# Two-layer hybrid decoder trunk on one core: the steps of the attention tasks one half unit further apart, branch B pairs every four half units

## The chip, the cores and the metric

The kernel runs on one core of a Trainium2 chip. The metric is device time in microseconds (us) of one execution, lower is better. PE is the matrix engine, DVE the vector engine, ACT the scalar engine, POOL and SP the two others; each works through its own list of instructions in the order in which the program wrote them, and waits for the others by semaphores.

## What is computed

Two layers, 256 tokens, model width 1024. Each layer is a half-step SwiGLU, a mixer, and a second half-step SwiGLU, each with a residual and a layer norm:

```python
for l in range(DEPTH):
    x = layer_norm(ALPHA * x + 0.5 * swiglu(x, ffn1_up[l], ffn1_down[l]), ln1_g[l], ln1_b[l])
    mix = hybrid_mixer(x, positions, w_in[l], ...)
    x = layer_norm(ALPHA * x + mix, ln2_g[l], ln2_b[l])
    x = layer_norm(ALPHA * x + 0.5 * swiglu(x, ffn2_up[l], ffn2_down[l]), ln3_g[l], ln3_b[l])
```

```python
s = jnp.einsum('bnqgrd,bnkgd->bngrqk', qb, kk) * (hd ** -0.5)     # banded_attention
s = jnp.where(mask[None, :, None, None], s, -jnp.inf)
m = jnp.max(s, axis=-1)                    # branch B: maximum with the sink as well
e = jnp.exp(s - m[..., None])
den = jnp.sum(e, axis=-1)                  # branch B: plus exp(sink - m)
o = jnp.einsum('bngrqk,bnkgd->bnqgrd', e, vv) / den_t[..., None]
lse = jnp.transpose(m, (0, 1, 4, 2, 3)) + jnp.log(den_t)
```

The mixer has three branches that are gated, summed and projected: A (12 heads, three dilated windows whose outputs are combined by their softmax denominators), B (16 query heads on 2 key heads, window 128, with a sink in the denominator) and C (retention, 8 heads). All is float32.

## The kernel before

Nearly all time goes to products of the activations with weights. Each weight is loaded as float32 (`ws`) and split into a high part `wh` (ACT, line 279) and a low part `wl` (DVE, line 289, `ws` minus `wh`); three products of 256 or 512 columns (line 320) then make one product of full precision. The weights are cut into units of up to four 128-row tiles by 512 columns, and each unit is worked through in two halves (`mm_unit(u, 0)` and `mm_unit(u, 1)`, for the two halves of the output). One such half is a half unit: 24 matmuls of 256 columns or 12 of 512. Within a unit `run` writes, in this order: the first half's matmuls and a `tick`; `hi_until`, which issues the `wh` of the unit three further on to ACT; the second half's matmuls and a `tick`; `lo_until`, which issues the `wl` of that same unit to DVE. So `wh` stands behind the steps of a first half's tick on ACT, and `wl` waits for that `wh`.

The attention is hung between the half units by hand. Each task is a generator, and one `tick` steps it to its next `yield`; a `yield` more puts what follows one half unit later in all five lists. The ends of a product chunk (`done_...`) are written right after the tick: the rotation of queries and keys (`rope`, four to five DVE instructions, lines 523 to 543) for the chunks `cq`, `ck`, `bq`, `bkv`, `aqk`; copies and a Silu on ACT for others.

- `b_pair` (branch B, eight pairs of heads in a layer, called here (0,0) to (1,3)): scores on PE into `S` (line 634), then on DVE the mask with a running maximum (639) and the negated maximum `bnm` (786), on ACT the exponentials (643) and the sink's (791). A `yield`. On DVE the reciprocal of the denominators `bden` (793, 794), on ACT the scaling of the probabilities (798). A `yield`. Four transposes on PE into `T` and their copy by ACT (625, 626). A `yield`. The last two. For every second pair a further `yield` and the product with the values, `U` (814), for two pairs, with its copy (816).
- `a_quad` (branch A, three in a layer): near scores of two head pairs (two yields behind each), far scores with their mask and exponentials, a `yield`, the merge of the two sums (`top`, `af`, `aw`, `fn`, lines 712 to 724), a `yield`, the scaling (730 and 734), a `yield`, three steps of transposes (625, 626, into `T` and `S`), two yields, the values (`U`, 748).

`T` and `U` have one buffer each in PSUM, `S` two. `an`, where the probabilities lie, has two buffers, `af` one. A pair starts when three half units have passed since the last start, a quad when no pair and no quad is under way.

Half units are counted here from the one after which the scores of pair (0,0) stand: that is 0. Even ones are first halves of a unit (a `wh` follows), odd ones second halves (a `wl` follows).

```
kind    b_pair scores at           a_quad starts at   values of the last quad at
before  0 3 6 9 12 15 18 21        25 44 60           71
```

Of the kernel before, what the change touches and what calls it, by code (L numbers as in the profile page):

```python
# [161 lines left out]
class Kernel:  # L162
# [40 lines left out]
    def tick(self, half):  # L203
        self.pairs = self.step(self.pairs)
        alive = self.step(self.tasks[half])
        kind = self.waiting and self.waiting[0][0] <= self.now and self.waiting[0][2]
        if kind and {"two": half == 1, "pair": self.now >= self.last + 3, "quad": not self.pairs}[kind]:
            g = self.waiting.popleft()[1]
            next(g)
            (alive if kind == "two" else self.pairs).append(g)  # L210
            self.last = self.now
        self.tasks[half] = alive + self.fresh
        self.fresh = []
        self.now += 1
# [480 lines left out]
    def a_quad(self, s):  # L695
        nc = self.nc
        new = lambda n: self.sml.tile([128, 2, 2, 4], F32, name=n, bufs=2)
        near, far, moved, f, w = (new(n) for n in ("near", "far", "moved", "af", "aw"))

        places = [(slice(32 * r, 32 * r + 32), t, slice(64 * (r % 2) + 32 * t, 64 * (r % 2) + 32 * t + 32), r // 2)  # L700
                  for r in range(4) for t in range(2)]
        P = []
        for b in range(2):
            P.append(self.near_scores(s, b, near))
            yield
            yield
        for rows, t, to, rp in places:
            nc.gpsimd.tensor_copy(moved[to, :, rp], near[rows, :, t])
        F = self.far_scores(s, far)
        yield  # L710
        top = self.sml.tile([128, 2, 4], F32, name="top", bufs=2)
        nc.vector.tensor_tensor(top, moved[:, 0], far[:, 0], op=OP.min)
        for g, x in enumerate((moved, far)):
            nc.vector.tensor_tensor(f[:, g], top, x[:, 0], op=OP.subtract)
        nc.scalar.activation(f, f, AF.Exp)
        for g, x in enumerate((moved, far)):
            nc.vector.tensor_tensor(w[:, g], f[:, g], x[:, 1], op=OP.mult)
        nc.vector.tensor_tensor(top, w[:, 0], w[:, 1], op=OP.add)
        nc.vector.reciprocal(top, top)
        for g in range(2):  # L720
            nc.vector.tensor_tensor(f[:, g], f[:, g], top, op=OP.mult)
        fn = self.sml.tile([128, 2, 4], F32, name="fn", bufs=2)
        for rows, t, to, rp in places:
            nc.scalar.activation(fn[rows, t], f[to, 0, rp], AF.Copy)  # L724
        yield
        for b in range(2):
            for e in range(2):
                for t in range(2):
                    sl = P[b][:, e, self.TILES[t]]
                    nc.scalar.activation(sl, sl, AF.Copy, scale=fn[:, t, 2 * b + e:2 * b + e + 1])  # L730
        for h in range(4):
            for rp in range(2):
                sl = F[:, 256 * h + 128 * rp:256 * h + 128 * rp + 128]
                nc.scalar.activation(sl, sl, AF.Copy, scale=f[:, 1, rp, h:h + 1])  # L734
        yield
        for x, n in ((P[0], 6), (P[1], 6), (F, 8)):
            x = x.rearrange("p e k -> p (e k)") if n == 6 else x
            self.transpose_p(x, 0, 4)
            self.transpose_p(x, 4, n, spare=True)
            yield  # L740
        yield
        self.a_values(s, P, F)
# [31 lines left out]
    def b_pair(self, n, b):  # L774

        nc, l = self.nc, self.layer
        Sp = self.pair_scores(self.bq[n][:, b], self.kb[:, n])
        P = self.b_p[n, b] = self.probs((4 * n + b) % 3 == 2)
        mx, nm, den, es = (self.sml.tile([128, 2, 2], F32, name=x) for x in ("bmx", "bnm", "bden", "bes"))
        h = 8 * n + 2 * b  # L780
        for e in range(2):
            sk = self.sink[:, l, h + e:h + e + 1]
            for t in range(2):
                self.masked(P[:, e, self.TILES[t]], Sp[e][:, self.TILES[t]], self.mask[:, 512 - 128 * t:640], mx[:, e, t:t + 1])
            nc.vector.tensor_scalar(mx[:, e], mx[:, e], 0.125, sk, op0=OP.mult, op1=OP.max)
        nc.vector.tensor_scalar(nm, mx, -1.0, None, op0=OP.mult)
        for e in range(2):
            sk = self.sink[:, l, h + e:h + e + 1]
            for t in range(2):
                self.exp(P[:, e, self.TILES[t]], nm[:, e, t:t + 1], den[:, e, t:t + 1])  # L790
            nc.scalar.activation(es[:, e], mx[:, e], AF.Exp, bias=sk, scale=-1.0)
        yield
        nc.vector.tensor_tensor(den, den, es, op=OP.add)
        nc.vector.reciprocal(den, den)
        for e in range(2):
            for t in range(2):
                sl = P[:, e, self.TILES[t]]
                nc.scalar.activation(sl, sl, AF.Copy, scale=den[:, e, t:t + 1])
        yield
        x = P.rearrange("p e k -> p (e k)")  # L800
        self.transpose_p(x, 0, 4)
        yield
        self.transpose_p(x, 4, 6)
        if b % 2 == 0:
            return
        yield
        U = self.p1.tile([128, 2, 256], F32, name="U")
        v = self.vb[:, :, 64 * n:64 * n + 64]
        for i in range(2):
            p = self.b_p[n, b - 1 + i]  # L810
            for j in range(2):
                for e in range(2):
                    u = U[64 * e:64 * e + 64, i]
                    nc.tensor.matmul(u[:, 128 * j:], v[:, j], p[:, e, 256 * j:256 + 128 * j], start=j == 0, stop=j == 1,
                                     skip_group_check=True)
        nc.scalar.activation(self.y[1][:, 4 * n + b - 1:4 * n + b + 1], U, AF.Copy)
        self.b_done += 1
# [279 lines left out]
```

## Time and profile before

| | |
|---|---|
| three runs | 1761.38, 1761.82 (median), 1762.82 us |
| the profiled execution | 1762.2 us, span 1760.0 us |
| PE busy | 1694.4 us, 96% of the span |
| PE's weight loads | 1543.4 us, 88% |
| DVE busy | 1067.1 us, 61% |
| ACT busy | 842.3 us, 48% |
| POOL busy | 96.1 us, 5% |
| mean granted clock of PE | 0.983 |

A share of busy time says which engine is nearest to its limit over the whole span. Which wait counts at a place is read from the list of waits, from the timeline of the engine that waits, and then from the timelines of those that it waits for.

### The profile page before, as it was taken

How to read it: one execution, taken by the hardware profiler on the slowest of the kernel's cores; microseconds unless marked ns; L12 is line 12 of the kernel's file. 1: busy time of each engine (PE TensorE's matmuls, PEld its weight loads, DVE VectorE, ACT ScalarE, POOL GpSimd, SP SyncE). 2: the span in 40 equal slices, each digit the busy share in tenths (PEclk: the TensorE clock that was granted, in tenths of full speed). 3: DMA queues.
4: the chain of work that ended last, by engine and by line, in shares of the span. 5: the costliest groups of instructions: out<-in, count | busy, mean ns of one | idle time of the engine just before them, and what ended most of it. 6: DMA issues, size and time to landing. Idle time of an engine off the chain costs nothing.

```text
span 1760.0 us, 29034 instructions
## 1 busy us (share of the span) xinstructions
PE 1694.4 (96%) x12325; PEld 1543.4 (88%) x12325; DVE 1067.1 (61%) x1536; ACT 842.3 (48%) x1207; POOL 96.1 (5%) x176
## 2 busy tenths in 40 slices
PE   9999999899988999999999999999999989999997
PEld 7998898788878998999899988978888889979985
DVE  5555677677564557555655546877666635675544
ACT  5444334675467444444344434366664574444431
POOL 0000001010210000000000000010102100000000
PEclk9999999999999999999999999999999999999998
DMA  7555543433443445555455465343344434555451
GB/s 288 210 185 194 207 169 125 142 135 138 161 159 117 180 180 192 209 210 204 165 188 206 176 222 193 144 144 120 132 144 156 156 144 180 194 185 213 172 206 48
DMA packets 49137, 303.38 MB, mean 172 GB/s; under 512 B 7024, under 2 KB 7280, under 8 KB 15088
## 3 DMA queue, kind: packets, MB, share of 16 engines
q1 hardware_dynamic: 44640, 294.12, 45.7%
q0 software_dynamic: 4224, 7.35, 1.2%
q8 instruction: 96, 1.57, 0.3%
q14 instruction: 33, 0.27, 0.0%
q10 hardware_dynamic: 144, 0.07, 0.0%
HBM read 297.31 MB, written 1.05 MB: 170 GB/s over the span
## 4 chain that ended last, share of the span: by engine, by line
PE 80%; DVE 9%; ACT 8%; issue 2%; DMA 0%; POOL 0%; SPq 0%; POOLq 0%; DVEq 0%; ACTq 0%
PE acc L320 75%; DVE wl L289 3%; ACT wh L279 2%; ACT an L643 1%; ACT af L643 1%; DVE an L639 1%; PE T L625 1%; PE S L634 1%; DVE af L639 1%; PE U L748 1%; ACT an L730 1%; ACT fn L724 1%; ACT af L734 1%; DVE rt L523 0%; DVE x L479 0%
## 5 line engine op out<-in xcount | busy, mean ns | idle before, releaser
L320 PE MATMUL acc<-xT,wh 128*128 128x256 f32 x4800 | 854.7, 281 | 0.0
L289 DVE TENSOR_TENSOR wl<-ws,wh 128x2048 fp32r<-128x2048 f32 (+1 forms) x277 | 615.5, 2241 | 215.2 <-ACT wh L279 213.5
L320 PEld LDWEIGHTS acc<-xT,wh 128*128 128x128 f32 x4800 | 740.7, 190 | 0.2
L320 PE MATMUL acc<-xT,wl 128*128 128x256 f32 x2400 | 683.3, 285 | 0.0
L279 ACT ACTIVATE wh<-ws 128x2048 fp32r<-128x2048 f32 (+1 forms) x277 | 518.8, 1874 | 249.8 <-PE acc L320 208.8
L320 PEld LDWEIGHTS acc<-xT,wl 128*128 128x128 f32 x2400 | 457.5, 191 | 8.2 <-issue 6.7
L320 PE MATMUL acc<-wh,xT 128*128 128x512 f32 (+1 forms) x832 | 265.9, 394 | 0.2
L320 PE MATMUL acc<-wh,hT 128*128 128x512 f32 x704 | 222.9, 396 | 0.0
L320 PEld LDWEIGHTS acc<-wh,xT 128*128 128x128 f32 x832 | 156.2, 190 | 37.3 <-issue 2.3
L320 PE MATMUL acc<-wl,xT 128*128 128x512 f32 (+1 forms) x416 | 162.2, 390 | 0.2 <-DVE wl L448 0.2
L320 PEld LDWEIGHTS acc<-wh,hT 128*128 128x128 f32 x704 | 132.6, 188 | 31.3
L320 PE MATMUL acc<-wl,hT 128*128 128x512 f32 x352 | 139.4, 396 | 0.0
L320 PE MATMUL acc<-slab,wh 128*128 128x256 f32 x704 | 123.8, 279 | 0.0
L490 DVE TENSOR_TENSOR h<-sa,acc 128x512 f32<-128x512 f32 x36 | 24.8, 688 | 154.2 <-PE acc L320 154.2
L320 PEld LDWEIGHTS acc<-slab,wh 128*128 128x128 f32 x704 | 107.2, 188 | 0.1
L320 PE MATMUL acc<-slab,wl 128*128 128x256 f32 x352 | 99.0, 281 | 0.0
L487 ACT ACTIVATE sa<-acc 128x512 f32<-128x512 f32 x36 | 21.5, 597 | 158.4 <-PE acc L320 158.4
L320 PEld LDWEIGHTS acc<-wl,xT 128*128 128x128 f32 x416 | 79.1, 190 | 16.4 <-DVE wl L448 0.5
L320 PEld LDWEIGHTS acc<-wl,hT 128*128 128x128 f32 x352 | 66.3, 188 | 15.5
L625 PE MATMUL T<-ident,an 128*128 128x128 f32 x120 | 26.5, 325 | 47.1 <-ACT an L730 26.3
L574 POOL DMA_DIRECT2D va<-slab x96 | 51.4, 538 | 324.6 <-ACT slab L570 319.7
L320 PEld LDWEIGHTS acc<-slab,wl 128*128 128x128 f32 x352 | 66.2, 188 | 1.6 <-issue 1.3
(177 smaller groups left out, 1242.3 us busy)
## 6 DMA issues: line engine op xcount, KB each, us to landing
ws<-in_w_dram SPq DMA_DIRECT2D x265, 1024.0 KB, 4.9
ws<-in_w_dram SPq DMA_DIRECT2D x12, 512.0 KB, 4.2
ws<-in_w_dram SPq DMA_DIRECT2D x12, 256.0 KB, 5.9
va<-slab POOLq DMA_DIRECT2D x96, 32.0 KB, 4.1
gain<-in_ln_g_dram SPq DMA_DIRECT2D x4, 512.0 KB, 5.8
gain<-in_ln_b_dram SPq DMA_DIRECT2D x4, 512.0 KB, 7.1
slab<-in_decay_dram POOLq DMA_DIRECT2D x4, 512.0 KB, 4.7
x<-in_x_dram SPq DMA_DIRECT2D x4, 256.0 KB, 5.8
```

What stands on the lines that cost most here:

```text
L279: self.nc.scalar.activation(wh[:, :n], self.staged[v][:, :n], AF.Copy)
L289: self.nc.vector.tensor_tensor(wl[:, :n], ws[:, :n], wh[:, :n].bitcast(F32), op=OP.subtract)
L320: nc.tensor.matmul(ps[:, c0:c1], a, b, start=first, stop=last, skip_group_check=len(parts) > 1)
L487: nc.scalar.activation(self.sa, ps, AF.Silu)
L490: nc.vector.tensor_tensor(h, self.sa, ps, op=OP.mult)
L574: nc.gpsimd.dma_start(self.vf[s][p0:p0 + 32, r], self.stage[r::4, t, g])
L625: nc.tensor.transpose(ps[:, 128 * (i - lo):128 * (i - lo) + 128], P[:, 128 * i:128 * i + 128], self.ident)
L634: self.nc.tensor.matmul(Sp[e][:, 128 * t:128 + 256 * t], q[r, 128 * t:128 * t + 128], k[r, :128 * t + 128], start=True, stop=True)
L639: self.nc.vector.tensor_tensor_reduce(out=P, in0=Sp, in1=mask, op0=OP.add, op1=OP.max, scale=1.0, scalar=-3e38, accum_out=mx)
L643: self.nc.scalar.activation(P, P, AF.Exp, bias=nm, scale=0.125, accum_out=den)
L724: nc.scalar.activation(fn[rows, t], f[to, 0, rp], AF.Copy)
L730: nc.scalar.activation(sl, sl, AF.Copy, scale=fn[:, t, 2 * b + e:2 * b + e + 1])
```

## The change

Five `yield`s are added and one number is raised.

```diff
-        if kind and {"two": half == 1, "pair": self.now >= self.last + 3, "quad": not self.pairs}[kind]:
+        if kind and {"two": half == 1, "pair": self.now >= self.last + 4, "quad": not self.pairs}[kind]:
...
         F = self.far_scores(s, far)
         yield
+        yield
         top = self.sml.tile([128, 2, 4], F32, name="top", bufs=2)
...
             nc.scalar.activation(fn[rows, t], f[to, 0, rp], AF.Copy)
         yield
+        yield
         for b in range(2):
...
                 nc.scalar.activation(sl, sl, AF.Copy, scale=f[:, 1, rp, h:h + 1])
+        yield
         yield
         for x, n in ((P[0], 6), (P[1], 6), (F, 8)):
...
             nc.scalar.activation(es[:, e], mx[:, e], AF.Exp, bias=sk, scale=-1.0)
         yield
+        yield
         nc.vector.tensor_tensor(den, den, es, op=OP.add)
...
                 nc.scalar.activation(sl, sl, AF.Copy, scale=den[:, e, t:t + 1])
         yield
+        yield
         x = P.rearrange("p e k -> p (e k)")
```

In a pair the scaling stands two half units behind the scores and not one, the first transposes four and not two; the step to the last transposes and the one to the values keep one half unit. In a quad the merge stands two behind the far scores, the scaling four and not two, the first transposes six and not three. Pairs start at 0, 4, 8, ... 28, quads at 34, 48 and 62, and the last quad's values stand at 76.

The lists of the two programs show what this moves. On ACT, around the last transposes of pair (0,3) and the values that need them (626: copies of transposes; 643, 791 or 794: exponentials of the next pair; 279: `wh`; 816 or 821: copy of the values' product). Before:

```order
L626 ACTIVATE an_3103<-T_3189 128x512
L626 ACTIVATE an_3103<-T_3222 128x256
L643 ACTIVATE an_3232,bden_3235<-an_3232,bnm_3234 128x128
L643 ACTIVATE an_3232,bden_3235<-an_3232,bnm_3234 128x256
L791 ACTIVATE bes_3236<-bmx_3233,sink_110 128x2
L643 ACTIVATE an_3232,bden_3235<-an_3232,bnm_3234 128x128
L643 ACTIVATE an_3232,bden_3235<-an_3232,bnm_3234 128x256
L791 ACTIVATE bes_3236<-bmx_3233,sink_110 128x2
L279 ACTIVATE wh_3258<-ws_3026 128x2048
L816 ACTIVATE y_2277<-U_3285 128x512
```

The same place now:

```order
L626 ACTIVATE an_3188<-T_3341 128x512
L643 ACTIVATE an_3353,bden_3356<-an_3353,bnm_3355 128x128
L643 ACTIVATE an_3353,bden_3356<-an_3353,bnm_3355 128x256
L794 ACTIVATE bes_3357<-bmx_3354,sink_110 128x2
L643 ACTIVATE an_3353,bden_3356<-an_3353,bnm_3355 128x128
L643 ACTIVATE an_3353,bden_3356<-an_3353,bnm_3355 128x256
L794 ACTIVATE bes_3357<-bmx_3354,sink_110 128x2
L279 ACTIVATE wh_3379<-ws_3150 128x2048
L626 ACTIVATE an_3188<-T_3406 128x256
L821 ACTIVATE y_2277<-U_3433 128x512
```

The copy of the last two transposes stood ahead of the next pair's exponentials and of a `wh`; now it stands behind both.

On ACT, in the second quad, from its far exponentials (643) to its scaling (715, 724 or 716, 725: the merge; 447: a split of branch B's result). Before:

```order
L643 ACTIVATE af,far<-af,far 128x128 x8
L279 ACTIVATE wh<-ws 128x2048
L715 ACTIVATE af<-af 128x16
L724 ACTIVATE fn<-af 32x4 x8
L730 ACTIVATE an<-an,fn 128x128
```

Now:

```order
L643 ACTIVATE af,far<-af,far 128x128 x8
L279 ACTIVATE wh<-ws 128x2048
L716 ACTIVATE af<-af 128x16
L725 ACTIVATE fn<-af 32x4 x8
L447 ACTIVATE slab<-y 128x512
L279 ACTIVATE wh<-ws 128x2048
L447 ACTIVATE slab<-y 128x512
L732 ACTIVATE an<-an,fn 128x128
```

A `wh` and two splits now stand between merge and scaling. On DVE, from the negated maximum of pair (0,3) (786 or 789) to its reciprocal (794 or 798), before:

```order
L786 TENSOR_SCALAR bnm<-bmx 128x4
L523 STREAM_SHUFFLE rt<-acc 128x512
L524 TENSOR_TENSOR rt<-acc,cos 128x512
L525 TENSOR_TENSOR rt<-rt,sin 128x512
L534 TENSOR_TENSOR slab<-rt 128x512
L289 TENSOR_TENSOR wl<-ws,wh 128x2048
L793 TENSOR_TENSOR bden<-bden,bes 128x4
L794 RECIPROCAL bden<-bden 128x4
```

Now:

```order
L789 TENSOR_SCALAR bnm<-bmx 128x4
L523 STREAM_SHUFFLE rt<-acc 128x512
L524 TENSOR_TENSOR rt<-acc,cos 128x512
L525 TENSOR_TENSOR rt<-rt,sin 128x512
L543 TENSOR_TENSOR slab<-rt 128x256 x2
L523 STREAM_SHUFFLE rt<-acc 128x512
L524 TENSOR_TENSOR rt<-acc,cos 128x512
L525 TENSOR_TENSOR rt<-rt,sin 128x512
L543 TENSOR_TENSOR slab<-rt 128x256 x2
L289 TENSOR_TENSOR wl<-ws,wh 128x2048
L797 TENSOR_TENSOR bden<-bden,bes 128x4
L798 RECIPROCAL bden<-bden 128x4
```

Both rotations of a chunk and a `wl` now stand between a pair's maximum and its reciprocal.

## Rows read from the trace of the kernel before

**Rows 1.** Busy time by stretch: PE, PEld, DVE, ACT, POOL, granted clock, DMA share, GB/s.

```profile
260.00:600.00 340.00, 315.18 (x2545) 284.38 (x2544) 220.28 (x485) 200.34 (x418) 39.83 (x76) 0.96 0.40 143
...
1130.00:1470.00 340.00, 314.91 (x2529) 283.98 (x2529) 219.66 (x484) 198.76 (x418) 39.86 (x76) 0.96 0.40 142
```

**Rows 2.** PE's waits over the whole span: us in total, times, longest.

```profile
PE T L625 <- ACT an L730: 26.3, 6, 4.5
PE T L625 <- ACT an L798: 12.6, 6, 2.5
PE T L625 <- ACT an L626: 7.7, 6, 1.5
```

**Rows 3.** Two stretches with waits, columns as in the first group.

```profile
360.00:380.00 20.00, 17.87 (x117) 14.34 (x116) 15.81 (x39) 12.04 (x33) 0.00 (x0) 1.00 0.41 155
...
420.00:440.00 20.00, 15.82 (x84) 13.71 (x83) 13.39 (x21) 14.83 (x33) 0.00 (x0) 0.83 0.41 149
```

**Rows 4.** The chain that ended last, first layer: start, us, what.

```profile
396.20 1.45 PE U L814 x16
...
411.01 1.10 PE S L678 x64
...
501.66 2.81 PE acc L320 x24
...
572.43 2.38 PE U L748 x48
```

**Rows 5.** The chain within 499 to 506 us: four transposes without a wait.

```profile
504.48 0.44 PE T L625 x4
```

**Rows 6.** Timeline of PE: scores of pair (0,0), first layer.

```profile
294.27 0.93 PE L634 MATMUL S<-kb,slab 64*128 64x128 f32 x8
```

**Rows 7.** Timeline of DVE around pair (1,0), 347.8 to 358.5 us.

```profile
345.68 2.29 DVE L289 TENSOR_TENSOR wl<-ws,wh 128x2048 fp32r<-128x2048 f32 x1 [3.43 <-ACT wh L279]
...
349.72 0.74 DVE L523 STREAM_SHUFFLE rt<-acc 128x512 f32<-128x512 f32 x1
...
352.75 0.16 DVE L793 TENSOR_TENSOR bden<-bden,bes 128x4 f32<-128x4 f32 x1
...
353.05 0.75 DVE L523 STREAM_SHUFFLE rt<-acc 128x512 f32<-128x512 f32 x1
...
356.09 2.28 DVE L289 TENSOR_TENSOR wl<-ws,wh 128x2048 fp32r<-128x2048 f32 x1
```

**Rows 8.** Timeline of ACT, the same pair.

```profile
351.98 1.91 ACT L279 ACTIVATE wh<-ws 128x2048 fp32r<-128x2048 f32 x1
...
354.27 1.48 ACT L798 ACTIVATE an<-an,bden 128x128 f32<-128x128 f32 x4
```

**Rows 9.** Values of branch B, 260 to 600 us: busy us, mean ns, idle before.

```profile
L814 PE MATMUL U<-an,vb 128*64 128x256 f32 (+1 forms) x48 | 4.7, 332 | 0.0
```

**Rows 10.** Timeline of ACT beside pair (0,0).

```profile
299.44 1.28 ACT L842 ACT_TABLE_LOAD   x1
```

**Rows 11.** Timeline of DVE in the second quad of the first layer.

```profile
476.03 0.28 DVE L639 CUSTOM_DVE_ANT_0 an<-S,mask 128x128 f32<-128x128 f32 x1
...
477.26 0.17 DVE L658 TENSOR_SCALAR near<-mx 128x4 f32<-128x4 f32 x1
481.16 2.29 DVE L289 TENSOR_TENSOR wl<-ws,wh 128x2048 fp32r<-128x2048 f32 x1 [3.74 <-ACT wh L279]
...
485.18 0.17 DVE L689 TENSOR_SCALAR far<-fx 128x8 f32<-128x8 f32 x1
```

**Rows 12.** Timeline of ACT in the same quad.

```profile
488.49 1.90 ACT L279 ACTIVATE wh<-ws 128x2048 fp32r<-128x2048 f32 x1
...
491.49 1.72 ACT L724 ACTIVATE fn<-af 32x4 f32<-32x4 f32 x8 [1.01 <-DVE af L721]
493.23 2.88 ACT L730 ACTIVATE an<-an,fn 128x128 f32<-128x128 f32 x8
...
500.15 0.57 ACT L626 ACTIVATE an<-T 128x512 f32<-128x512 f32 x1
```

## The prediction, made before the changed kernel ran

> **What bounds it now.** I read the busy times by stretch first. In the two stretches that hold the attention PE is busy 315.2 and 314.9 of 340 us [rows 1], so it idles 24.8 and 25.1 us there; DVE is busy 65% and ACT 59%. The list of PE's waits puts all of this on one line: transposes of probabilities that ACT has not yet scaled (26.3 us in quads, 12.6 in pairs), or whose one `T` buffer ACT has not yet copied out (7.7) [rows 2]. Then the clock by stretch: after a wait of over 4 us in a quad 20 us show a granted clock of 0.83, so a share of them at the lower of its two levels (1.2 instead of 2.4 GHz); 360 to 380 us, which hold a wait of a pair, show 1.00 [rows 3]. PE is the bound and the change adds no work to it; what it alters is these waits.
>
> What a layer's stretch loses in all is read from two ends: pair (0,0)'s scores start at 294.27 us [rows 6], the last quad's values end at 572.43 + 2.38 = 574.81 [rows 4], 280.5 us with 71 half units between. At full clock a half unit takes 2.81 us [rows 4], 71 take 199.5. A pair adds scores 0.93, four transposes 0.44 and two 0.22 [rows 5, 6], 1.6; eight pairs make 12.7, four products with values at 1.45 make 5.8, and a quad makes 7.5 (two near scores 1.86, far scores 1.10, 20 transposes 2.2, values 2.38), three 22.5 [rows 4 to 6]. Together 240.5, so **40 us a layer are lost**: 25 idle, the rest at the lower clock and in transposes that wait for one slice after another.
>
> **What the change does.** It removes nothing and adds no instruction; it moves steps to later places in the lists of PE, ACT and DVE. SP's list and POOL's DMA issues carry on as before: the first quad's values are through eight half units before its `vf` buffer is filled again, and no task is left to the drain ahead of branch A's gate. PE reaches the transposes two half units later in pairs and three in quads, 5.6 and 8.4 us, more than any wait in the list (4.5). If the steps on ACT and DVE were done as early as now, all waits would go. They are not: each moves down its list too, behind a `wh`, a `wl` and rotations. Two rows show what that does. DVE idles 3.43 us before `wl` for ACT's `wh`, and 3.74 in a quad [rows 7, 11], while the masks of the next step stand behind that `wl`. Masks, exponentials, `wh`, `wl`, next masks form **one ring through two engines that take turns**. It closes when the step stands at an even half unit, whose `wh` follows the step on ACT. With pairs every three half units every second pair stood at an odd one; now all pairs and all three quads stand at even ones.
>
> **Pairs.** The ring of a pair beside a rotated chunk, from masks to masks: masks 1.8 (from the end of a `wl` to 349.72), two rotations at 3.04 (353.05 to 356.09), `wl` 2.2, reciprocal 0.3 [rows 7], scaling 1.5, `wh` 1.8 [rows 8], and the `wl` that waits for it 2.2: 15.9 us. PE's own work in four half units is 11.24 + 1.6, with half a product of values 13.6. So over two pairs PE must wait 31.8 − 27.1 = 4.7 us. It waits where it first needs the ring: at the values, since the copy of the last two transposes now stands behind the next pair's exponentials (2.2 from 349.8) and a `wh` [rows 7, 8]. With the ring's lag those masks start 5.4 us after PE came to the scores; masks, exponentials, `wh` and copy take 6.4 with hand-offs, PE needs 8.1 to the values: 3.7 us there, and the rest, some 0.8, at the next transposes. Now this product never waits [rows 9]. It happens for (0,1), (0,3) and (1,1); (1,3) has no pair behind it. Pair (0,1) is later still, beside the Silu: from the end of its scores 3.2 until a late `wl` has ended, masks 1.9, exponentials 2.2, a table load 1.3 [rows 10], Silu 0.5, `wh` 1.8, a copy and the second Silu 0.9, a product and a `wl` on DVE 2.9, reciprocal and first slice 0.7, hand-offs 0.5: 15.9 against 4 × 2.81 + 0.22 = 11.5 on PE, a wait of 4.4, with 0.6 more between its slices 5.0. Pair (0,0) by the same chain 1.9. Pairs: 1.9 + 5.0 + 3 × 3.7 + 2 × 0.8 = **19.6 us**.
>
> **Quads.** The second, from the end of its first near scores: masks 1.4 [rows 11], two rotations and a `wl` 8.3 (9.7); near masks again (11.1), exponentials and `wh` 3.7 (481.16 less 477.43; 14.8), `wl` (17.0), far masks 1.95 (19.0), then rotations and `wl` on DVE 8.3 (27.3), while the far exponentials and `wh` end at 24. Merge 1.7 and `fn` 1.75 (30.8) [rows 12], a split 0.5, `wh` 1.8, a split 0.5 (33.6), first slice 0.4: 34.0. PE comes after ten half units and two scores at 30.1: 4 us of wait, and 1.0 between slices. The rest of the scaling ends at 38.6; split, copy, `wh`, split, copy (4 at about 0.5 like [rows 12], 1.8) and the copy of `T` end at 43, PE comes to the next transposes at 38.4: 4.6. Sum 9.7. The first quad by the same steps: 0.7 for `S` at the far scores, 0.8 for a late `wl`, 4.0, 1.0 and 2.8, so 9.3; the third, with no rotations, 3.5 + 1.0 + 2.8. Quads **26.3**, all 45.9 us.
>
> The same chains laid out in the order of before give 14.1 for the pairs and 25.1 for the quads, 39.2, where the trace lost 40. So I take the difference of the two layouts, 45.9 − 39.2 = 6.7 us a layer, and 2 × 6.7 = 13.4 us in both. From the profiled execution's 1762.2 us (its span 1760.0 and 2.2 around it; 0.4 above the median of the runs, 1761.82) that makes **1776 us**. The one price that the trace does not show is the new wait at the values: between 0, as now [rows 9], and 3.7; I take 3.7, since the ring has to be paid somewhere. At 0 it would be 11.1 a layer less, 1753.
>
> **Rivals.** *The spacing outlasts the queues* (12%). For it: the engines have room, 65 and 59% busy. It decides itself at the ring: were it under PE's 13.6 us (the `wl` not behind the exponentials), the transposes would find their slices. Then up to 35 of the 40 us of each layer go, half of it or all: 1727 to 1692 us, faster. The Trainium skill, Perfetto Trace Analysis, section Identifying the Most-Contended Engine, has the engine with the highest occupancy as the bound, for ACT and DVE by occupancy itself; by that rule neither binds at 65% and this rival would hold. Against it stand the two waits of DVE for `wh`: neither engine is full, and the ring binds all the same.
>
> *The ring holds, but the values do not wait* (10%): 1753 as above, a little faster or the same.
>
> *The clock falls at each new wait* (10%). Five waits of a layer are new or grown past 3 us; if each is followed by a lower clock, PE loses what it may behind a quad's wait: of 20 us at 0.83 some 6.8 are at half clock, and were PE busy through all of them 3.4 would be lost [rows 3]. Five more in each of two layers: up to 34 us, 1810. I give it little since PE is paced by the ring there and would only wait less. The Trainium skill, TensorE: Matmul & The Clock Gate, section HAM oscillation, tells of a loop in which the wait of every round threw the engine back to its low clock. The row at 1.00 holds a wait that did not.
>
> **How the numbers follow.** My forecast has 68%. Range 1757 to 1792: below it lie the first rival and the end of the second, above it the upper half of the clock's 34 us. A measurement can tell 0.2%, 3.5 us. Slower by more: forecast and clock, 0.78. Faster: the first rival and half of the second, 0.17. The same: its other half, 0.05.
>
> **What would show it.** In the changed profile PE's busy time stays near 1694 us. Right: the values of branch B appear in the list of waits for ACT's copy (626), three times a layer, near 3.7 us; the transposes still wait for both scalings, the longest near 4 us; DVE still idles 3 us and more before `wl`; pairs beside rotations are near 16 us apart. Wrong: the waits for the scalings vanish, the clock is 1.00 throughout both attention stretches, or the values do not wait.

## The result, and the profile after

The changed kernel took **1771.57 us** (median of 4 runs, 1771.28 to 1772.75) against 1761.66 (4 runs, 1761.38 to 1762.82) of the kernel before: ratio 1.0056, 95% interval 1.0039 to 1.0074. That is slower by more than the 0.2% that a measurement can tell, and inside the range 1757 to 1792; the forecast was 1776. The profiled execution took 1771.4 us with a span of 1769.3, against 1762.2 and 1760.0.

Busy time by stretch of the changed kernel, columns as in [rows 1, 3]:

```profile
260.00:600.00 340.00, 315.50 (x2494) 282.32 (x2493) 214.34 (x482) 195.78 (x414) 38.35 (x76) 0.96 0.40 142
360.00:380.00 20.00, 17.76 (x95) 13.78 (x94) 15.70 (x36) 9.88 (x21) 0.00 (x0) 0.91 0.36 129
420.00:440.00 20.00, 19.72 (x115) 15.38 (x116) 13.08 (x24) 9.86 (x18) 0.00 (x0) 1.00 0.44 158
1130.00:1470.00 340.00, 314.35 (x2493) 280.54 (x2492) 217.76 (x485) 191.74 (x408) 38.37 (x76) 0.96 0.39 139
```

PE idles as much as it did, while DVE went down from 65% to 63% and ACT from 59% to 58%: space was added, and the two engines that PE waits for do a little less in the same 340 us. PE's waits over the whole span, as [rows 2]:

```profile
PE T L625 <- ACT an L732: 12.2, 4, 3.6
PE T L625 <- ACT an L802: 10.2, 8, 2.5
PE T L625 <- ACT an L626: 8.0, 6, 1.7
PE acc L320 <- ACT slab L447: 7.2, 4, 3.4
PE U L819 <- ACT an L626: 6.7, 3, 2.2
PE U L819 <- ACT af L626: 2.2, 2, 1.1
PE acc L320 <- DVE wl L289: 1.3, 2, 0.7
```

The waits for a quad's scaling (L730 before, L732 now) fell from 26.3 to 12.2 us. In their place stand waits that the list did not have: branch B's values for the copy (8.9 us), and branch B's projection for its split `slab` (7.2), which stands on ACT behind the second quad's merge (`fn`) and ahead of its scaling.

The ring can be read straight off DVE. Timeline of DVE in the changed kernel, from the masks of pair (0,3) to those of pair (1,0): start, us, operation, and in brackets the idle time before it.

```profile
344.56 2.29 DVE L289 TENSOR_TENSOR wl<-ws,wh 128x2048 fp32r<-128x2048 f32 x1 [3.43 <-ACT wh L279]
...
348.51 0.17 DVE L789 TENSOR_SCALAR bnm<-bmx 128x4 f32<-128x4 f32 x1
...
354.64 2.28 DVE L289 TENSOR_TENSOR wl<-ws,wh 128x2048 fp32r<-128x2048 f32 x1
...
357.03 0.18 DVE L798 RECIPROCAL bden<-bden 128x4 f32<-128x4 f32 x1
360.63 2.29 DVE L289 TENSOR_TENSOR wl<-ws,wh 128x2048 fp32r<-128x2048 f32 x1 [3.42 <-ACT wh L279]
...
364.58 0.17 DVE L789 TENSOR_SCALAR bnm<-bmx 128x4 f32<-128x4 f32 x1
```

Timeline of ACT in the same piece:

```profile
348.71 0.40 ACT L643 ACTIVATE an<-an,bnm 128x128 f32<-128x128 f32 x1 [3.52 <-DVE bnm L789]
...
350.86 1.91 ACT L279 ACTIVATE wh<-ws 128x2048 fp32r<-128x2048 f32 x1
...
357.31 1.49 ACT L802 ACTIVATE an<-an,bden 128x128 f32<-128x128 f32 x4 [4.28 <-DVE bden L798]
358.70 1.90 ACT L279 ACTIVATE wh<-ws 128x2048 fp32r<-128x2048 f32 x1
```

Read the two together. DVE writes the negated maximum (348.51), and ACT, which idled 3.52 us for them, runs the exponentials. DVE finishes its rotations and a `wl` and gives the reciprocal (357.03), for which ACT idled 4.28 us. ACT scales, then runs the `wh` behind the scaling (358.70); DVE idled 3.42 us for that and runs its `wl`, and only then come the masks of the next pair (364.58). Each engine stands still while the other works. From maximum to maximum it is 16.07 us here; the neighbours, 332.89 to 348.51 and 364.58 to 380.63, took 15.62 and 16.05. The forecast had 15.9.

Between 260 and 600 us DVE's waits of `wl` for `wh`, first in the kernel before, then in the changed one (us in total, times, longest), read:

```profile
DVE wl L289 <- ACT wh L279: 50.5, 14, 7.2
```

```profile
DVE wl L289 <- ACT wh L279: 77.8, 20, 5.1
```

The two ends of the attention stretch, which [rows 4, 6] showed of before, are these in the changed kernel (timeline of PE, then the chain that ended last):

```profile
294.34 0.93 PE L634 MATMUL S<-kb,slab 64*128 64x128 f32 x8
```

```profile
593.50 2.38 PE U L751 x48
```

That is 301.54 us with 76 half units. By the same sum as before (76 × 2.81 + 41.0), and 0.9 for transposes of `y` that now fall into the stretch, 255.5 us of it are work: **46.0 us are lost** in layer 1, and 46.1 in layer 2 (1168.50 to 1470.10). The kernel before lost 40.0 in layer 1 and, by the same two ends (1162.91 to 1445.36), 41.9 in layer 2. The difference is 6.0 and 4.2 us, 10.2 together, beside the 9.3 by which the span grew. So the time lies in the attention stretches.

### The profile page after: what moved, and what is told of

Same layout as the page of the kernel before. It is cut to its first block, busy times and chain, and to the rows that moved or that the text cites. A ratio compares the mean times of both kernels' runs of the same rounds, so it can differ in the third digit from the quotient of the medians.

```text
span 1769.3 us, 29021 instructions
## 1 busy us (share of the span) xinstructions
PE 1702.9 (96%) x12325; PEld 1546.8 (87%) x12325; DVE 1064.7 (60%) x1536; ACT 840.0 (47%) x1207; POOL 93.1 (5%) x176
## 4 chain that ended last, share of the span: by engine, by line
PE 66%; DVE 17%; ACT 13%; issue 3%; DMA 0%; POOL 0%; SPq 0%; POOLq 0%; ACTq 0%
PE acc L320 63%; DVE wl L289 6%; ACT wh L279 5%; DVE an L639 1%; DVE slab L543 1%; ACT an L643 1%; DVE rt L523 1%; DVE rt L525 1%; DVE rt L524 1%; ACT an L802 1%; ACT af L643 1%; ACT an L732 1%; PE U L751 1%; ACT af L736 1%; DVE af L639 1%
## 5 line engine op out<-in xcount | busy, mean ns | idle before, releaser
L320 PE MATMUL acc<-slab,wh 128*128 128x256 f32 x704 | 127.6, 285 | 0.9 <-DVE slab L448 0.6
L320 PEld LDWEIGHTS acc<-wl,xT 128*128 128x128 f32 x416 | 79.6, 191 | 16.7 <-DVE wl L448 0.5
L320 PEld LDWEIGHTS acc<-wl,hT 128*128 128x128 f32 x352 | 66.2, 188 | 15.6
L625 PE MATMUL T<-ident,an 128*128 128x128 f32 x120 | 25.6, 317 | 31.1 <-ACT an L732 12.2
```

The costliest lines, as they stand in the source:

```text
L320: nc.tensor.matmul(ps[:, c0:c1], a, b, start=first, stop=last, skip_group_check=len(parts) > 1)
L625: nc.tensor.transpose(ps[:, 128 * (i - lo):128 * (i - lo) + 128], P[:, 128 * i:128 * i + 128], self.ident)
```

## The experiments

The theory: the ring closes because all steps stand at even half units, with a `wh` behind the step on ACT. The rivals: the added space itself costs, in longer chains or buffers held longer; or single waits, such as the one at the values, each cost what they show. Each run stands beside the kernel before on the same chip, 1763.01 us with the first four and 1763.24 with the others. The changed kernel's 1771.57 us stands beside 1761.66, so differences to it are good to some 2 us.

**1. The changed kernel with every step one half unit later (e1_odd).**

```diff
     def queue(self, gen, kind):
...
-        self.waiting.append((self.now + 2, gen, kind))
+        self.waiting.append((self.now + (3 if kind == "pair" else 2), gen, kind))
```

> The changed kernel with the first pair one half unit later, so that all pairs (1, 5, 9, ... 29) and all quads (35, 49, 63) stand at odd half units; spacings as in the change. Theory (the ring: a step at an even half unit puts its exponentials ahead of a wh, the wl waits for that wh, and the next masks wait for that wl): at odd half units the wh that a wl needs is already ahead of the step, the ring is open, and the spacing then does what it can. Of 46 us lost a layer some 10 to 12 stay, most of them around the second quad, whose transposes meet the splits of branch B's result: 1771.6 less 2 x 35, about 1702 us, 1695 to 1715. The values of branch B wait under 1 us. Rival (the steps have simply too much ahead of them in full lists, whatever half unit they stand at): 1772 us, within 5. Rival (low clock sets it): the clock stretches stay, over 1765.

It took **1710.06 us** (ratio to before 0.9701, interval 0.9686 to 0.9715), inside the interval expected. Same steps, same spacing, same period, 61.5 us less than the changed kernel. PE's waits over the span and DVE's between 260 and 600 us:

```profile
PE T L625 <- ACT an L626: 7.0, 2, 3.5
PE acc L320 <- ACT slab L447: 2.5, 2, 1.3
PE T L625 <- ACT an L732: 1.6, 2, 0.8
```

```profile
DVE wl L289 <- ACT wh L279: 12.4, 6, 5.3
```

The waits for the pairs' scaling and at the values are gone, DVE's wait for `wh` is down from 77.8 to 12.4 us. Timeline of DVE beside a pair's exponentials and scaling in this run:

```profile
352.98 0.17 DVE L789 TENSOR_SCALAR bnm<-bmx 128x4 f32<-128x4 f32 x1
...
356.08 2.28 DVE L289 TENSOR_TENSOR wl<-ws,wh 128x2048 fp32r<-128x2048 f32 x1
...
358.57 2.28 DVE L289 TENSOR_TENSOR wl<-ws,wh 128x2048 fp32r<-128x2048 f32 x1
```

Neither `wl` waits now. The `wh` of the first ran on ACT at 347.20, well ahead of this pair's exponentials, and that of the second at 355.59, right behind them, while DVE was still at the first. The scores of the pairs follow each other at some 12.9 and 14.6 us by turns; PE's own work without and with a product of values is 12.8 and 14.3. And in the stretch from 260 to 600 us both engines are busier than in the slower kernels:

```profile
260.00:600.00 340.00, 333.03 (x2764) 305.26 (x2763) 231.86 (x495) 213.07 (x429) 40.52 (x76) 0.99 0.44 159
```

DVE stands at 68% and ACT at 63%, and PE waits for them less. What is still lost lies elsewhere than expected: by the table at the end of this section the third quad, not the second, holds most of it, 9.5 us of 14.8. Its transposes wait 3.5 us for ACT's copy of `T`, which stands behind two activations of the gate and a `wh`.

**2. The changed kernel with `wh` ahead of the steps (e2_wh_first).** The half units stay even; only ACT's list changes.

```diff
+                if name == "mix":
+                    self.hi_until(u + 3)
                 self.mm_unit(u, 0, tick=True)
                 self.hi_until(u + 3)
```

> The changed kernel, all steps where they are, but within the mixer each unit's wh is issued to ACT before the first half's matmuls and tick, so ahead of the steps at an even half unit and not behind them. Theory (ring): the wl no longer waits for the exponentials, the ring is cut at one link: about 1700 us, 1693 to 1715, and DVE's waits for wh in 260 to 600 us fall from 77.8 us to under 40. Rival (full lists): the same work stands in the same lists, 1772 us within 5.

It took **1712.78 us** (ratio 0.9713, 0.9699 to 0.9728), 59 us less than the changed kernel and inside the interval expected, which ended at 1715. The waits of PE and, between 260 and 600 us, of DVE:

```profile
PE T L625 <- ACT an L626: 11.9, 4, 4.5
PE T L625 <- ACT an L802: 3.9, 2, 1.9
```

```profile
DVE wl L289 <- ACT wh L279: 13.0, 5, 4.2
```

Two different edits, one of the steps' places and one of `wh` alone, open the ring and give the same time within 3 us. What they share is that the next `wl` behind a step's masks on DVE needs a `wh` that stands ahead of that step's exponentials on ACT. But only the pairs and the first quad gain by both. With `wh` first the second quad still loses 8.9 us (3.4 at odd half units), where its copy of `T` stands on ACT behind splits and a `wh` (the wait of 4.5 us); the third loses 2.6 (9.5 at odd half units). That the two totals agree so closely is partly chance.

**3 and 4. Each half of the change alone (e3_pairs_only, e4_quads_only).** The first takes back the three added half units in the quads (behind the far scores, the merge and the scaling; two are shown); the second adds these three to the kernel before.

```diff
         F = self.far_scores(s, far)
         yield
-        yield
...
         for rows, t, to, rp in places:
             nc.scalar.activation(fn[rows, t], f[to, 0, rp], AF.Copy)
         yield
-        yield
```

> Only the pairs are changed (two yields and every four half units); the quads keep the spacing of before and start at 34, 45 and 60. Theory (ring): pairs lose 20 us a layer and not 14.6; of the quads the first, which stood at 25 (odd) before, now stands at 34 (even) and loses as the two others of before did, 9 and not 7, and the second, at 45 (odd), some 7 and not 9: 5 us more a layer, about 1772 us, 1767 to 1778. Rival (each spacing helps its own steps): faster than before, under 1757.

> Only the quads are changed (three yields); the pairs are those of before, the quads start at 25, 44 and 60. Theory (ring): the first quad has all its steps at odd half units and loses some 2 us in place of 7, the second and third stay at even ones and lose 9 and 7, as in the changed kernel, in place of 9 and 9: 7 us less a layer, about 1748 us, 1742 to 1755. Rival (the spacing of the quads costs what the pairs' does): 1766 or more. Rival (spacing helps every quad): under 1735.

Pairs alone: 1777.16 us (ratio 1.0080, 1.0063 to 1.0096). Quads alone: **1742.86** (0.9884, 0.9869 to 0.9899). Both lie inside the intervals expected, the second near its lower end. So the harm comes with the pairs' half of the change, and the spacing of the quads by itself pays 20 us. Of the 8.5 us that pairs alone lose more in layer 1, 5.6 are the pairs' own; the first quad, now at an even half unit without the added space, loses 4.9 more (12.3 in place of 7.4), and the second, now at an odd one, 2.2 less. The two do not add: +14.2 and −20.1 make −6, where the change gave +9.9. The first quad shows why. In layer 1 it takes 47.3 us from its near scores to its values where it starts at half unit 25 (quads alone) and 47.4 at 35 (first run), and 56.1 in the changed kernel, where it starts at 34. By taking the pairs to period four, the change also puts this quad on an even half unit.

**5. The kernel before with `wh` first (e5_before_wh_first).** The edit of the second run, without the change.

```diff
+                if name == "mix":
+                    self.hi_until(u + 3)
                 self.mm_unit(u, 0, tick=True)
                 self.hi_until(u + 3)
```

> The kernel before, its steps and pairs untouched, with one edit: in the mixed phase the `wh` of a unit is put on ACT ahead of the unit's first half, where it stood behind that half's steps. Ring theory: what costs is `wh` behind the exponentials and scalings, with or without the added space; the queues laid out by hand lose 27.4 us a layer in place of 39.2, 23.6 us less in two layers, so about 1738 us (1730 to 1748), and DVE's waits of `wl` for `wh` between 260 and 600 us fall from 50.5 to under 20. Rival, the space is what makes the other order pay, since in the kernel before a scaling is wanted one half unit after its scores whatever `wh` does: 1755 to 1764, with the waits at the transposes near the 49 us they have.

It took **1739.64 us** (ratio 0.9864, 0.9849 to 0.9879), 2 us from the forecast; DVE's waits of `wl` for `wh` came down to 20.6 us, just above the 20 expected. Waits of PE, and of DVE between 260 and 600 us:

```profile
PE T L625 <- ACT an L730: 14.4, 6, 2.8
PE T L625 <- ACT an L798: 10.6, 8, 1.9
PE T L625 <- ACT an L626: 4.5, 4, 1.4
```

```profile
DVE wl L289 <- ACT wh L279: 20.6, 7, 6.4
```

Now compare the same change on the two orders of `wh`: with `wh` behind the step the added space costs 9.9 us (1761.66 to 1771.57); with `wh` ahead of it the same space **gains 27 us** (1739.64 to 1712.78, and both runs have the kernel before within 0.3 us). The space was not the fault. Most of it could not be used while the ring was closed: beside the pairs it cost 5.4 us in layer 1 with `wh` behind the step (14.6 to 20.0) and gained 7.9 with `wh` ahead (13.3 to 5.4).

**6. The values two half units later (e6_values_later).** In the changed kernel, two more half units between a pair's transposes and its values; quads move to 36, 50 and 64, still even.

```diff
         if b % 2 == 0:
             return
         yield
+        yield
+        yield
         U = self.p1.tile([128, 2, 256], F32, name="U")
```

> The changed kernel with two more half units between the transposes and the values of a branch B pair, so that the values no longer wait for ACT's copy; steps and quads stay on even half units, quads two later. Ring theory: the ring sets the pace of the pairs beside rotations, so what U gives back (some 4.5 us a layer) returns at the next pair's transposes: from pair (0,0)'s scores to the first quad's, where 134.1 us held 34 half units, 36 half units take 139 to 141 us; and with the quads two half units later the layout loses 2.7 us more a layer: 1771 to 1779 us. Rival, the wait at the values is a cost of its own: that stretch takes 135 to 137 us, and the time is 1758 to 1767.

It took 1784.60 us (ratio 1.0122, 1.0105 to 1.0139), above the 1771 to 1779 expected. The waits of PE:

```profile
PE T L625 <- ACT an L802: 20.6, 11, 2.6
PE T L921 <- ACT an L626: 17.6, 4, 8.4
```

The waits at the values are gone, and those for the pairs' scaling doubled, from 10.2 to 20.6 us. From pair (0,0)'s scores to the first quad's are 142.2 us in layer 1, where two half units on 134.1 make 139.7: nothing was gained, as the ring theory says, and 2.5 us were lost. The rest of the miss is a new wait: the transposes of `y` (`yT_task`), which begin with a gate chunk wherever the quads stand, now meet the third quad's transposes at the `T` buffer (8.4 us in a layer). By the table the third quad loses 17.7 us in place of 7.3, while the first loses 4.4 in place of 9.2 at a half unit that is still even. The theory had neither.

**7. Both remedies at once (e7_odd_wh_first).** The edits of the first and the second run together.

```diff
-        self.waiting.append((self.now + 2, gen, kind))
+        self.waiting.append((self.now + (3 if kind == "pair" else 2), gen, kind))
...
+                if name == "mix":
+                    self.hi_until(u + 3)
                 self.mm_unit(u, 0, tick=True)
```

> Both remedies at once: pairs and quads on odd half units, and `wh` on ACT ahead of the unit's first half. Ring theory: each opens the same ring, so they don't add; on odd half units `wh` already stood clear of the steps, and put earlier it now stands between a step's exponentials and the wait behind it: laid out by hand 17.9 us a layer in place of 11.4, some 13 us more than the odd half units alone, about 1722 us (1712 to 1730). Rival, they are two separate costs, and each takes its own part away: 1690 to 1705, below either alone.

It took 1724.08 us (ratio 0.9778, 0.9763 to 0.9792), 14 us more than odd half units alone and near the 1722 expected. Two remedies for one ring do not add; the second puts a `wh` where it was not in the way, and pairs, second and third quad each lose 2 to 3 us a layer more.

**8. Pairs every three half units, with the added space (e8_every_three).**

```diff
-        if kind and {"two": half == 1, "pair": self.now >= self.last + 4, "quad": not self.pairs}[kind]:
+        if kind and {"two": half == 1, "pair": self.now >= self.last + 3, "quad": not self.pairs}[kind]:
```

> The changed kernel with branch B's pairs taken up every three half units again, the added space kept: pairs then stand on even and odd half units by turns, the first quad on an odd one (27), the others on even ones (44 and 60). Ring theory: half of the pairs and the first quad leave the ring; laid out by hand 27.4 us a layer in place of 46.0, 37 us less in two layers, about 1735 us (1725 to 1750). Rival, the space itself is what costs (more steps at once, buffers held longer), and pairs packed closer make it worse: 1770 or more. Second rival, the longer period is harmless either way: within 5 us of the changed kernel.

It took 1748.48 us (ratio 0.9914, 0.9896 to 0.9932), inside what the theory expected, near its upper end, and 23 us less than the changed kernel. PE now waits at another place:

```profile
PE T L625 <- ACT an L626: 27.1, 10, 5.7
PE T L625 <- ACT an L802: 1.7, 2, 0.9
```

The scaling is there in time; the one `T` buffer, which ACT copies out behind the exponentials of a neighbouring pair, is not. About half of the 27.1 us is the pairs', the other half the quads'. The time came as the theory had it, but not from where: half of the pairs were to leave the ring, and the pairs still lose 18.4 us in place of 20.0. What was gained is the first quad's (9.2 to 0.6) and part of the second's (9.6 to 6.1). That the pairs are held by the `T` buffer now is read from these waits only; no run gave them a second buffer.

The stretch of layer 1 in all kernels, by the two ends used above. "Lost" is the stretch less the half units at 2.81 us and 41.0 us, or 41.9 from 76 half units on, where 8 and more transposes of `y` fall in; it is good to about 1 us. Behind it stand its parts by the same sum: the pairs, from pair (0,0)'s scores to the first quad's (18.5 us of work beside 25, 34, 36 or 27 half units), and each quad from its first scores to the end of its values (7.5 us beside 11 or 14; 8.4 for the third where the transposes of `y` fall in):

```
kernel              stretch  half units  lost   pairs  quads 1, 2, 3      time
before               280.5      71       40.0    14.6   7.4  9.0   8.9    1761.7
changed              301.5      76       46.0    20.0   9.2  9.6   7.3    1771.6
odd half units       270.3      76       14.8     1.6   0.6  3.4   9.5    1710.1
wh first             272.8      76       17.3     5.4   0.6  8.9   2.6    1712.8
pairs only           289.0      71       48.5    20.2  12.3  6.8   8.9    1777.2
quads only           280.8      74       31.9    16.2   0.5  6.1   8.9    1742.9
before, wh first     271.5      71       31.0    13.3   6.7  5.0   5.8    1739.6
values later         315.0      78       53.9    22.6   4.4  9.4  17.7    1784.6
odd and wh first     277.3      76       21.8     4.2   0.6  5.4  11.8    1724.1
every three          284.5      74       35.5    18.4   0.6  6.1  10.1    1748.5
```

The times follow the lost column, two layers to a kernel: from the changed kernel to odd half units it is 2 × 31.2 = 62.4 us, measured 61.5. The ring accounts for most of that: 18.4 us of the 31.2 are the pairs', 8.6 the first quad's. The second and the third quad follow it only in part.

## Why the prediction was right

**What bounds it.** Right: PE stays the bound and its waits are what changes. They are set by two engines at 63 and 58% that take turns, and opening the ring took most of them away (PE's idle time from 24.5 to 7.0 us of 340 in the first run). The Trainium skill, Perfetto Trace Analysis, section Identifying the Most-Contended Engine, measures how near ACT and DVE are to their limit by occupancy. That does not show this ring: from the changed kernel to the one at odd half units DVE goes up from 63 to 68% and ACT from 58 to 63, and the time falls.

**Moved steps move in each queue.** Right. PE came two and three half units later, and waited as long as before (24.5 us of 340 in place of 24.8), since masks, exponentials and scaling had moved behind the next `wh` and `wl` as well.

**The ring and the even half units.** Right, and the central point. Its pace, forecast 15.9 us, was 15.6 to 16.07. That the parity decides was shown by the first run, that it acts through the place of `wh` by the second, for the pairs and the first quad. For the second and third quad it is not shown: each gained by one of the two edits and little or nothing by the other.

**Pairs, 19.6 us.** The sum was right: layer 1 lost 20.0 up to the first quad's scores. Its parts were not. I had 3.7 us at the values three times a layer. The trace shows none for (0,1) in layer 1, 2.24 for (0,3) and 1.06 for (1,1), and half the 5.0 us at the transposes of (0,1). Timeline of PE from the scores of (1,0) to the values of (0,3), and of DVE at the masks of (1,0):

```profile
358.71 0.93 PE L634 MATMUL S<-kb,slab 64*128 64x128 f32 x8
...
365.61 0.87 PE L819 MATMUL U<-af,vb 128*64 128x256 f32 x8
366.31 0.59 PE L819 MATMUL U<-an,vb 128*64 128x256 f32 x2
369.15 0.86 PE L819 MATMUL U<-an,vb 128*64 128x256 f32 x6 [2.24 <-ACT an L626]
```

```profile
362.84 0.28 DVE L639 CUSTOM_DVE_ANT_0 an<-S,mask 128x128 f32<-128x128 f32 x1
```

Masks to copy took 6.3 us (forecast 6.4), and PE came to the first matmul that needs the copy 8.2 us after the scores (8.1). The term that was off is the lag: the masks start 4.1 us after PE comes to the scores, not 5.4. In other places PE idles less because it came later: after the wait of 2.48 us before 326.07 the records have a granted clock of 0.50, the lower of the two levels, for 6.8 us, and the values of (0,1) come late enough not to wait. In layer 2 those transposes wait 1.11 us and the values 2.23. The sum is the same, 20.0 in both layers, and over two pairs PE lost 4.3 us from (0,2) to (1,0) and 4.8 from (1,0) to (1,2), where the ring asks for 4.7. What the ring asks for, PE pays in idle time or in slow work. That is also why PE's busy time did not stay near 1694 us:

```profile
PE 1702.9 (96%) x12325; PEld 1546.8 (87%) x12325; DVE 1064.7 (60%) x1536; ACT 840.0 (47%) x1207; POOL 93.1 (5%) x176
```

It grew by 8.5 us. The four groups of branch B's values took 5.5 us more (16.3 to 21.8) and the pairs' scores 2.3; the other groups rose and fell by up to 4 and nearly cancel. PE's idle time in the two attention stretches stayed at some 50 us. Busy time of a matmul that is drawn out is lost time too; the two ends of the stretch count it, the list of waits doesn't.

**Quads, 26.3 us.** Measured 26.0 to 26.1, and each one as forecast: 9.2, 9.6 and 7.3 for 9.3, 9.7 and 7.3. The places within them differ: the second quad's wait came one step earlier than I had it, at the projection's matmuls (3.42 us for `slab`), and the third waited 2.53 + 1.55 for the forecast 3.5 + 2.8.

**The sum.** The layout of the changed order was good to 0.2 us (45.9 forecast, 46.0 and 46.1 measured). **The mis-sized term is the layout of the order before**, 39.2, from which I took the difference in place of what the trace lost. The trace lost 40.0 in layer 1, as the prediction says, and 41.9 in layer 2, which I had not read out. Most of the miss is beside the pairs: laid out 14.1, lost 14.6 in layer 1 and 16.7 in layer 2. PE's waits there are the same in both layers, but layer 2 has two stretches at a granted clock of 0.50 (1211.7 to 1215.1 and 1249.3 to 1252.6 us), layer 1 one (303.8 to 307.1). With 40.0 and 41.9 the sum is (45.9 − 40.0) + (45.9 − 41.9) = 9.9 us, and 9.9 was measured, where I had 13.4. Agreement to a tenth is chance: by the two ends of the stretches the difference was 10.2, by the span 9.3.

**The rivals.** *The spacing outlasts the queues* fell as long as the ring is closed, and gave the right price for an open one: it put the time at 1692 to 1727, and the two kernels with an open ring took 1710 and 1713. *The values do not wait* (1753) was wrong in its price rather than in its condition: their waits came to 8.9 us in place of some 22, and the time did not fall by the rest; the sixth run took them away altogether and gained nothing. *The clock falls at each new wait*: the mean clock is 0.983 in both kernels. Single places differ both ways, 360 to 380 us from 1.00 to 0.91, and 420 to 440 from 0.83 to 1.00.

## What to carry to other kernels

A step that is moved in the program moves in the queue of every engine that it uses; space between steps paid here mainly where no periodic job, such as the `wh` and `wl`, tied these queues into a ring. Look for two engines that are both part idle and wait for each other by turns, lay out one round by hand, and ask where in the period of the side job the steps stand: one half unit, or one line of issue order, was worth 60 us here, six times what the change itself did. Then read the loss by parts: two edits with nearly the same time can leave it in different places. And judge an added space only after the ring is open, for the same edit cost 10 us before and gained 27 behind it.

## What the runs showed of the hardware that was not expected

Nearly equal idle time did not give an equal clock: in the kernel before, 20 us with 2.1 us of idle PE show a granted clock of 1.00 [rows 3]; in the changed one the same 20 us with 2.2 us idle show 0.91. Nor did equal waits: in layer 2 of the kernel before, waits of 1.74 and 2.08 us (at 1210.53 and 1248.42) stand beside stretches at 0.50, while in layer 1 the same two waits, 1.74 and 2.06 us (at 342.80 and 379.23), have 1.00 all around. In the fastest kernel only one stretch of layer 1's attention shows the lower level (548.75 us, for 6.8), and the mean clock rose from 0.983 in the kernel before to 0.995.
